# Local attention in a one-core hybrid block: scaling the output of a step instead of its probabilities

## The chip, the core and the metric

The kernel runs on one core of a Trainium2 chip. The metric is the device time of one execution in microseconds (us). Five engines work side by side, each with a queue of its own that runs in order: TensorE (PE in the profile; PEld is its loading of weights), VectorE (DVE), ScalarE (ACT), GpSimd (POOL) and SyncE (SP), which here only issues DMAs.

## The reference

One layer over 1024 latent tokens and 256 context tokens, width 1024, all in float32. A modulated norm feeds one projection; three token mixers work on it (A: attention in a window with a sink, B: global attention, C: a linear recurrence); their outputs are gated, merged and projected, and a gated MLP with a convolution follows. The change is in mixer A, with eight query heads of width 64 that share two key/value heads:

```python
s_loc = jnp.where(valid, s_loc, NEG_BIG)               # |kpos - qpos| <= 128
p = softmax(concatenate([s_ctx, s_loc, s_sink], -1))   # 256 context + up to 384 window keys + sink
o = p[..., :n_ctx] @ cv + p[..., n_ctx:-1] @ v_window  # the sink takes weight, gives no value
```

## The kernel before, in words

`attention` (L1229) runs once for mixer A (`br == 0`) and once for mixer B (`br == 1`). Each run has 16 steps: 8 blocks of 128 queries times 2 groups of 4 heads. In the trace mixer A's steps lie from about 697 to 889 us, mixer B's lead follows, and its steps end near 1222 us.

A step has three parts, which `weave` (L1214) interleaves in the order in which they are written down: `scores` of step it+1, `values` of step it, and a share of the gate projections (`gz`, L199 to L201), which need nothing of attention and fill TensorE. The framework's planner then orders each engine's queue from priorities and from times that it models. `qprep` (L1275) loads and transposes the queries two steps ahead.

- `softmax_window` (L1374) is the local `scores`. For each of four heads it makes five matmuls into a `sa` tile of PSUM (L1387 to L1392), takes the negative maximum (L1395, L1397), and writes `exp` to `pw` with its row sum (L1399). Then, per head (`NB = 1`, L68), it adds the sink's share to the sum (L1404 to L1406), takes the reciprocal (L1407), and GpSimd multiplies the whole 128x512 or 128x640 tile of probabilities by it (L1409).
- `softmax_global` (L1413) is mixer B's. It leaves its probabilities unscaled, makes one reciprocal per four heads, copies it out to 64 columns a head on GpSimd (L1450, tag `yT`) and puts that tile into `rs`.
- `values` (L1299) serves both. For each key tile, TensorE transposes four heads' probabilities into `pp` (L1321), a bank of the tag `a`; ScalarE makes the rounded half `ph` (L1325), VectorE the remainder `pl` (L1326), and two matmuls (L1307, L1308) add to `po`. At the end ScalarE copies the halves of `po` that have to change partitions (L1337, L1338), VectorE adds them to `yT` (L1341), and SP stores `yT` to DRAM (L1344). If `rs` has an entry for the step, two plain matmuls with the identity turn that tile into `pr`, also a bank of tag `a` (L1316), ahead of the third key tile; ScalarE copies `pr` to `ytmp` (L1318), and VectorE multiplies `yT` by it (L1343).

Tag `a` has two banks, shared by `pp`, `pr`, the turned queries `pq` (L1286) and, in a lead, `kt`. Tags `yT` and `ytmp` have two buffers each. The loads of keys and values for mixer B (L1251) stand behind mixer A's last store in SP's queue.

Of the kernel before, what the change touches and what calls it, by code (L numbers as in the profile page):

```python
# [12 lines left out]
AF = mybir.ActivationFunctionType  # L13
ALU = mybir.AluOpType
# [4 lines left out]
P = 128  # L19
# [48 lines left out]
NB = 1  # L68
# [1160 lines left out]
def attention(tc, nc, ap_, br, ins, kv_d, q_d, y_d, mm2, bank, ident, identr, fill_gen, fill_steps):  # L1229
    V, A, G, T, SP = nc.vector, nc.scalar, nc.gpsimd, nc.tensor, nc.sync  # L1230

    def tl(shape, tag, nm, bufs=2, dt=F32):
        return ap_.tile(shape, dt, tag=tag, name=f"{tag}{br}_{nm}", bufs=bufs)

    NK = 10
    KH = tl([P, 2, NK * P], "KH", 0, 1, F32R)
    KL = tl([P, 2, NK * P], "KL", 0, 1, F32R)
    VHL = tl([P, NK, 2, 2, 64], "VHL", 0, 1, F32R)
    if br == 0:
        tri = tl([P, 3 * P], "tri", 0, 1, F32)  # L1240
        SP.dma_start(tri, ins["tri"])
        trir = tl([P, 3 * P], "trir", 0, 1, F32R)
        A.copy(trir, tri)
        snk = tl([P, 8], "snk", 0, 1)
        SP.dma_start(snk, ins["sink"].to_broadcast([P, 8]))
        nsnk = tl([P, 8], "nsnk", 0, 1)
# [44 lines left out]
    def scores(it):  # L1291
        tt, g = divmod(it, 2)
        QT = QTs.pop(it)
        if br == 0:
            yield from softmax_window(nc, tl, mm2, tt, g, f"{it}_", QT, KH, KL, trir, identr, snk, nsnk, res)
        else:
            yield from softmax_global(nc, tl, mm2, g, f"{it}_", QT, KH, KL, res, rs)

# [49 lines left out]
    res, rs = {}, {}  # L1348
    def lead():
        for k0 in range(0, NK, 2):  # L1350
            prep(k0)
            yield
        qprep(0)
        qprep(1)
        yield
        yield from scores(0)
# [6 lines left out]
    for it in range(n_it):  # L1363
        PT, kts = res.pop(it)
        if it + 2 < n_it:
            qprep(it + 2)
        a, b = (min(fill_steps, int(fill_steps * i / (n_it - SKEW[br]))) for i in (it, it + 1))
        weave((scores(it + 1), S_LEN * (4 + br)) if it + 1 < n_it else (None, 0),
              (values(it, PT, kts), len(kts) + 1),
              (some(fill_gen, b - a), b - a))  # L1370
    man.close()


def softmax_window(nc, tl, mm2, tt, g, nm, QT, KH, KL, trir, identr, snk, nsnk, res):  # L1374
    V, A, G, T = nc.vector, nc.scalar, nc.gpsimd, nc.tensor
    lo, hi = max(tt - 1, 0), min(tt + 1, LT - 1)
    kts = [0, 1] + [2 + b for b in range(lo, hi + 1)]
    nk = len(kts) * P
    w = nk - 256
    m0 = (lo - (tt - 1)) * P  # L1380
    Ps = []
    st = tl([P, 8, 4], "st", nm)
    ng, sm, sk = st[:, 0], st[:, 1], st[:, 2]
    for h in range(4):

        sc = mm2(f"sa{nm}{h}").rearrange("p a b -> p (a b)")[:, 256:256 + nk]
        T.matmul(sc[:, :256], QT[:, h], KH[:, g, :256], start=True, stop=False)  # L1387
        T.matmul(sc[:, :256], QT[:, h], KL[:, g, :256], start=False, stop=True)
        k = (2 + lo) * P
        T.matmul(sc[:, 256:], QT[:, h], KH[:, g, k:k + w], start=True, stop=False)  # L1390
        T.matmul(sc[:, 256:], QT[:, h], KL[:, g, k:k + w], start=False, stop=False)
        T.matmul(sc[:, 256:], identr, trir[:, m0:m0 + w], start=False, stop=True)  # L1392
        n1 = ng[:, h:h + 1]
        hs = g * 4 + h
        V.tensor_reduce(out=n1, in_=sc, axis=AX.X, op=ALU.max, negate=True)  # L1395

        V.tensor_tensor(out=n1, in0=n1, in1=nsnk[:, hs:hs + 1], op=ALU.min)  # L1397
        pw = tl([P, 640], "pw", f"{nm}{h}", 8)
        A.activation(pw[:, :nk], sc, AF.Exp, bias=n1, accum_out=sm[:, h:h + 1])  # L1399
        Ps.append(pw)  # L1400
        if h % NB == NB - 1:
            b = slice(h - NB + 1, h + 1)
            bs = slice(hs - NB + 1, hs + 1)
            V.tensor_tensor(out=sk[:, b], in0=snk[:, bs], in1=ng[:, b], op=ALU.add)  # L1404
            A.activation(sk[:, b], sk[:, b], AF.Exp)
            V.tensor_tensor(out=sm[:, b], in0=sm[:, b], in1=sk[:, b], op=ALU.add)  # L1406
            V.reciprocal(sm[:, b], sm[:, b])  # L1407
            for j in range(h - NB + 1, h + 1):
                G.tensor_scalar(out=Ps[j][:, :nk], in0=Ps[j][:, :nk], scalar1=sm[:, j:j + 1], scalar2=1.0,  # L1409
                                op0=ALU.mult, op1=ALU.mult)  # L1410
        yield
    res[2 * tt + g] = ((lambda h, n: Ps[h][:, n * P:(n + 1) * P]), kts)


# [162 lines left out]
```

## Time and profile before

| | us |
|---|---|
| median of 3 runs (2128.03 to 2130.79) | 2129.37 |
| the profiled execution | 2129.82 |
| its span in the profile | 2127.9 |
| TensorE busy in the span | 2085.8 (98%) |
| GpSimd busy in the span | 288.1 (14%) |

Busy times of matmuls overlap, since a matmul begins before the one ahead of it has drained: read the distance from start to start beside them. "Idle before" is the gap of an engine, with the instruction that ended it.

### The profile page before, as it was taken

To read this page: it belongs to the slowest core of one execution; us is meant where nothing else is said; L and a number is where in the kernel's file an instruction comes from. 1 tells how busy PE (TensorE), PEld (TensorE's weight loads), DVE (VectorE), ACT (ScalarE), POOL (GpSimd) and SP (SyncE) were. 2 spreads that over 40 slices of the span, in tenths; PEclk is the share of its full clock that TensorE was granted. 3 is DMA by queue.
4 is the path that set the end of the run, shared out by engine and by line. 5 is a ranking of instruction groups with operands and counts; after the bars stand their busy time and mean duration, and the time that the engine had idled before them with its cause. 6 is when DMAs were issued, how large, how long until landed. Compare 5 with 4: busy or idle time off the path is not lost.

```text
span 2127.9 us, 30555 instructions
## 1 busy us (share of the span) xinstructions
PE 2085.8 (98%) x11686; PEld 1743.1 (82%) x11686; DVE 1380.5 (65%) x2299; ACT 1001.2 (47%) x1761; POOL 288.1 (14%) x257
## 2 busy tenths in 40 slices
PE   7999999999999999999999999999999999999997
PEld 4888888888988888878888788888888888888887
DVE  4736756636665777678887746569777777664423
ACT  4333333311123777678888734346445544453222
POOL 0000000010021222100000000011333344100111
PEclk9999999999999999999999999999999999999999
DMA  9511111136543211211100354641222222285342
GB/s 359 207 44 36 46 50 41 46 113 214 186 137 123 78 59 41 80 55 35 35 28 28 115 200 142 194 156 55 99 79 89 80 80 88 81 287 201 109 126 86
DMA packets 95490, 229.28 MB, mean 108 GB/s; under 512 B 10736, under 2 KB 35824, under 8 KB 94320
## 3 DMA queue, kind: packets, MB, share of 16 engines
q1 hardware_dynamic: 95344, 227.33, 32.1%
q8 instruction: 92, 1.51, 0.3%
q14 instruction: 54, 0.44, 0.1%
HBM read 181.68 MB, written 45.61 MB: 107 GB/s over the span
## 4 chain that ended last, share of the span: by engine, by line
PE 69%; DVE 3%; ACT 2%; issue 1%; DMA 1%; POOL 1%; SPq 0%; DVEq 0%; ACTq 0%; POOLq 0%
PE pp L1321 4%; PE gz L199 3%; PE dn L929 3%; PE dn L928 3%; PE dn L930 3%; PE gz L200 3%; PE gz L201 3%; PE up L852 2%; PE up L853 2%; PE up L854 2%; PE po L1307 2%; PE po L1308 2%; PE br L200 2%; PE br L201 2%; PE br L199 2%; PE upd L853 2%
## 5 line engine op out<-in xcount | busy, mean ns | idle before, releaser
L175 ACT CAST wh<-wr 128x1024 fp32r<-128x1024 f32 (+1 forms) x139 | 145.1, 1044 | 398.7 <-PE dn L929 69.1
L176 DVE TENSOR_TENSOR wl<-wr,wh 128x1024 fp32r<-128x1024 f32 (+1 forms) x139 | 171.1, 1232 | 221.1 <-ACT wh L175 206.7
L1326 DVE TENSOR_TENSOR pl<-pp,ph 128x512 fp32r<-128x512 f32 x236 | 159.3, 687 | 29.2 <-ACT ph L1325 23.5
L199 PE MATMUL gz<-hh,wh 128*128 128x512 f32 x384 | 156.3, 408 | 3.1 <-ACT gs L523 3.1
L1325 ACT CAST ph<-pp 128x512 fp32r<-128x512 f32 x236 | 135.7, 587 | 37.4 <-PE pp L1321 35.3
L201 PE MATMUL gz<-hh,wl 128*128 128x512 f32 x384 | 152.3, 397 | 0.0
L200 PE MATMUL gz<-hl,wh 128*128 128x512 f32 x384 | 152.1, 396 | 0.0
L210 PE MATMUL tm<-wl,hh 128*128 128x256 f32 x384 | 108.9, 283 | 3.3 <-DVE wl L176 3.3
L209 PE MATMUL tm<-wh,hh 128*128 128x256 f32 x384 | 108.9, 284 | 0.9 <-ACT qo L615 0.9
L211 PE MATMUL tm<-wh,hl 128*128 128x256 f32 x384 | 108.6, 283 | 0.0
L1307 PE MATMUL po<-ph,VHL 128*128 128x512 f32 x236 | 106.1, 450 | 1.4 <-ACT ph L1325 1.0
L929 PE MATMUL dn<-ac,wh 128*128 128x512 f32 x256 | 99.7, 390 | 0.0
L930 PE MATMUL dn<-ac,wl 128*128 128x512 f32 x256 | 99.6, 389 | 0.0
L928 PE MATMUL dn<-ac,wh 128*128 128x512 f32 x256 | 99.6, 390 | 0.0
L1308 PE MATMUL po<-pl,VHL 128*128 128x512 f32 x236 | 97.1, 411 | 0.1
L199 PEld LDWEIGHTS gz<-hh,wh 128*128 128x128 f32 x384 | 72.7, 189 | 17.2 <-ACT gs L523 5.2
L201 PEld LDWEIGHTS gz<-hh,wl 128*128 128x128 f32 x384 | 72.5, 189 | 15.0
L200 PEld LDWEIGHTS gz<-hl,wh 128*128 128x128 f32 x384 | 72.8, 190 | 11.6
L210 PEld LDWEIGHTS tm<-wl,hh 128*128 128x128 f32 x384 | 73.7, 192 | 4.3 <-DVE wl L176 4.0
L1321 PE MATMUL pp<-ident,plat 128*128 128x128 f32 x512 | 76.6, 273 | 0.0
L1321 PEld LDWEIGHTS pp<-ident,plat 128*128 128x128 f32 x512 | 62.7, 140 | 16.9 <-DVE pl L1326 1.2
L199 PE MATMUL br<-yh,wh 128*128 128x512 f32 x192 | 74.3, 390 | 1.6 <-ACT yh L1468 1.6
(1420 smaller groups left out, 5898.7 us busy)
## 6 DMA issues: line engine op xcount, KB each, us to landing
wr<-in_w_cm SPq DMA_DIRECT2D x48, 512.0 KB, 3.7
wr<-in_w_up SPq DMA_DIRECT2D x44, 512.0 KB, 3.5
wr<-in_w_down SPq DMA_DIRECT2D x33, 512.0 KB, 3.5
wmr<-in_w_mod SPq DMA_DIRECT2D x32, 512.0 KB, 4.5
gate_d<-gs SPq DMA_DIRECT2D x48, 256.0 KB, 2.3
sgt<-gate_d SPq DMA_DIRECT2D x24, 512.0 KB, 3.4
act_d<-u SPq DMA_DIRECT2D x22, 512.0 KB, 2.6
st<-act_d SPq DMA_DIRECT2D x44, 256.0 KB, 4.5
```

Of the source, the lines that this page charges most:

```text
L175: A.copy(hi[:, :n], raw[:, :n])
L176: (lo_eng or V).tensor_tensor(out=lo[:, :n], in0=raw[:, :n], in1=hi[:, :n].bitcast(F32), op=ALU.subtract)
L199: T.matmul(psl, wh[:, k, c], hh[:, k0 + k, cols], start=s, stop=False)
L200: T.matmul(psl, wh[:, k, c], hl[:, k0 + k, cols], start=False, stop=False)
L201: T.matmul(psl, wl[:, k, c], hh[:, k0 + k, cols], start=False, stop=e)
L210: T.matmul(psl, hh[:, k, toks], wl[:, k % 4, :], start=False, stop=False)
L928: T.matmul(z, w[0][:, c], h[0], start=s, stop=False)
L929: T.matmul(z, w[0][:, c], h[1], start=False, stop=False)
L930: T.matmul(z, w[1][:, c], h[0], start=False, stop=e)
L1307: T.matmul(po, vv, ph, start=n == 0, stop=False)
L1321: T.transpose(pp[:, h], PT(h, n), ident)
L1326: V.tensor_tensor(out=pl, in0=pp, in1=ph.bitcast(F32), op=ALU.subtract)
```

## The change: what it does

Local attention leaves its probabilities unscaled, as mixer B does. The sink's exponential, the addition and the reciprocal run once for four heads on 128x4 tiles; the reciprocal is copied out on GpSimd and put into `rs`. `values` is unchanged as text, and takes its `rs` path for mixer A too.

```diff
-            yield from softmax_window(..., snk, nsnk, res)
+            yield from softmax_window(..., snk, nsnk, res, rs)
...
         A.activation(pw[:, :nk], sc, AF.Exp, bias=n1, accum_out=sm[:, h:h + 1])
         Ps.append(pw)
-        if h % NB == NB - 1:
-            b = slice(h - NB + 1, h + 1)
-            bs = slice(hs - NB + 1, hs + 1)
-            V.tensor_tensor(out=sk[:, b], in0=snk[:, bs], in1=ng[:, b], op=ALU.add)
-            A.activation(sk[:, b], sk[:, b], AF.Exp)
-            V.tensor_tensor(out=sm[:, b], in0=sm[:, b], in1=sk[:, b], op=ALU.add)
-            V.reciprocal(sm[:, b], sm[:, b])
-            for j in range(h - NB + 1, h + 1):
-                G.tensor_scalar(out=Ps[j][:, :nk], in0=Ps[j][:, :nk], scalar1=sm[:, j:j + 1], scalar2=1.0,
-                                op0=ALU.mult, op1=ALU.mult)
         yield
+
+    V.tensor_tensor(out=sk, in0=snk[:, g * 4:g * 4 + 4], in1=ng, op=ALU.add)
+    A.activation(sk, sk, AF.Exp)
+    V.tensor_tensor(out=sm, in0=sm, in1=sk, op=ALU.add)
+    V.reciprocal(sm, sm)
+    rb = tl([P, 4, 64], "yT", f"r{nm}")
+    G.tensor_copy(rb, sm[:, :, None].to_broadcast([P, 4, 64]))
+    rs[2 * tt + g] = rb.rearrange("p a b -> p (a b)")
     res[2 * tt + g] = ((lambda h, n: Ps[h][:, n * P:(n + 1) * P]), kts)
```

## Rows read from the trace of the kernel before

**Rows 1.** The page, part 1: busy us, share of the span, instructions.

```profile
PE 2085.8 (98%) x11686; PEld 1743.1 (82%) x11686; DVE 1380.5 (65%) x2299; ACT 1001.2 (47%) x1761; POOL 288.1 (14%) x257
```

**Rows 2.** Busy time by stretch; the header names the columns.

```profile
core 0: us, PE busy (x) PEld busy (x) DVE busy (x) ACT busy (x) POOL busy (x), PEclk, DMA share, GB/s
697.00:706.00 9.00, 8.49 (x51) 7.01 (x50) 3.97 (x14) 6.43 (x15) 0.71 (x1) 1.00 0.35 116
706.00:730.00 24.00, 23.69 (x141) 19.36 (x140) 19.05 (x65) 18.31 (x50) 8.06 (x11) 1.00 0.23 67
730.00:874.00 144.00, 143.26 (x858) 124.41 (x857) 114.52 (x345) 104.65 (x264) 38.08 (x48) 1.00 0.16 49
874.00:886.00 12.00, 10.79 (x63) 8.56 (x61) 9.21 (x27) 8.91 (x23) 2.78 (x4) 1.00 0.21 47
888.00:892.00 4.00, 4.00 (x19) 3.33 (x18) 0.85 (x2) 0.42 (x1) 0.00 (x0) 1.00 0.41 130
908.00:927.00 19.00, 17.48 (x92) 13.57 (x91) 11.38 (x18) 13.93 (x29) 0.40 (x1) 1.00 0.17 56
```

**Rows 3.** Timeline of TensorE in mixer B, around a `pr` without a wait: start, us.

```profile
926.87 0.40 PE L199 MATMUL gz<-hh,wh 128*128 128x512 f32 x1
927.10 0.61 PE L1316 MATMUL pr<-ident,yT_r__8966 128*128 128x128 f32 x4
927.46 0.48 PE L1308 MATMUL po<-pl,VHL 128*128 128x512 f32 x1
927.78 0.60 PE L1321 MATMUL pp<-ident,plat 128*128 128x128 f32 x4
```

**Rows 4.** Groups of instructions by line, 697 to 889 us: busy, mean ns, idle before.

```profile
L1321 PE MATMUL pp<-ident,pw 128*128 128x128 f32 x304 | 47.3, 274 | 1.0 <-ACT QT L1288 0.7
```

**Rows 5.** Timeline of mixer A, TensorE at the end of a step.

```profile
743.26 0.28 PE L1388 MATMUL sa<-KL,QT 128*128 128x256 f32 x1
743.73 0.55 PE L1321 MATMUL pp<-ident,pw 128*128 128x128 f32 x3 [0.18 <-ACT QT L1288]
```

**Rows 6.** Waits of TensorE's weight loads, 697 to 889 us: total, times, longest.

```profile
PEld pp L1321 <- ACT QT L1288: 1.6, 4, 0.4
PEld pp L1321 <- POOL pw L1409: 1.1, 4, 0.3
```

**Rows 7.** Instructions of one step or one kind: min/median/max ns, first and last start.

```profile
L1409 POOL TENSOR_SCALAR pw<-pw,st__6758 x4: 799/808/812, 747.4 to 753.1; 128x640 f32<-128x640 f32 x4
L1407 DVE RECIPROCAL st__6758<-st__6758 x4: 149/158/165, 747.1 to 752.8; 128x1 f32<-128x1 f32 x4
L1407 DVE RECIPROCAL st__8168<-st__8168 x4: 151/157/164, 853.7 to 859.4; 128x1 f32<-128x1 f32 x4
L1405 ACT ACTIVATE st__6758<-st__6758 x4: 199/202/212, 745.5 to 752.3; 128x1 f32<-128x1 f32 x4
L1450 POOL COPY yT_r__8966<-st__8871 x1: 397/397/397, 924.5 to 924.5; 128x256 f32<-128x256 f32 x1
L1318 ACT COPY ytmp_R<-pr x16: 366/373/382, 929.6 to 1204.8; 128x256 f32<-128x256 f32 x16
L1343 DVE TENSOR_TENSOR yT<-yT,ytmp_R x16: 414/418/426, 943.7 to 1221.4; 128x256 f32<-128x256 f32 x16
```

**Rows 8.** Timeline of TensorE in mixer B, around a `pr` that waits for its bank.

```profile
1073.42 0.39 PE L201 MATMUL gz<-hh,wl 128*128 128x512 f32 x1
1074.10 0.68 PE L1316 MATMUL pr<-ident,yT_r__10632 128*128 128x128 f32 x4 [0.29 <-DVE pl L1326]
1074.54 0.48 PE L1307 MATMUL po<-ph,VHL 128*128 128x512 f32 x1
```

**Rows 9.** Timeline, last step of mixer A and SP's next issue.

```profile
879.12 0.19 ACT L1399 ACTIVATION_READ_ACCUMULATOR pw<-sa,st__8469 128x1 f32 x1
...
879.99 0.69 POOL L1409 TENSOR_SCALAR pw<-pw,st__8469 128x512 f32<-128x512 f32 x1 [1.49 <-DVE st__8469 L1407]
...
880.37 1.13 PE L1321 MATMUL pp<-ident,pw 128*128 128x128 f32 x8
880.66 1.05 ACT L175 CAST wh<-wr 128x1024 fp32r<-128x1024 f32 x1
...
882.24 0.50 PE L1307 MATMUL po<-ph,VHL 128*128 128x512 f32 x1 [0.74 <-ACT ph L1325]
...
888.91 0.37 SPq L1344 DMA_DIRECT2D y_d<-yT  x1
889.37 0.96 SPq L1251 DMA_DIRECT2D qf_kv<-kv_d  x2
```

More of the change, by code (lines that the diff above doesn't have):

```diff
@@ L1294, in scores @@
         if br == 0:
-            yield from softmax_window(nc, tl, mm2, tt, g, f"{it}_", QT, KH, KL, trir, identr, snk, nsnk, res)
+            yield from softmax_window(nc, tl, mm2, tt, g, f"{it}_", QT, KH, KL, trir, identr, snk, nsnk, res, rs)
         else:
@@ L1371, in attention, with softmax_window @@
     man.close()
-def softmax_window(nc, tl, mm2, tt, g, nm, QT, KH, KL, trir, identr, snk, nsnk, res):
+def softmax_window(nc, tl, mm2, tt, g, nm, QT, KH, KL, trir, identr, snk, nsnk, res, rs):
     V, A, G, T = nc.vector, nc.scalar, nc.gpsimd, nc.tensor
```

## The prediction, made before the result was known

> **What bounds the kernel now.** I read the page's busy shares first, then busy time by stretch for the part of the trace that holds mixer A, then who waits for whom there, and last the timeline of TensorE, start to start.
>
> Over the whole span TensorE is busy 98% and GpSimd 14% [rows 1]. The stage that the change touches is no exception. From 730 to 874 us, some twelve of the sixteen steps, TensorE is busy 143.26 of 144 us; with the stretches ahead and behind, idle time from 697 to 886 us comes to 0.51 + 0.31 + 0.74 + 1.21 = 2.8 us [rows 2]. VectorE is at 80% there, ScalarE at 73%, GpSimd at 26%. The granted clock is 1.00 in every stretch, the 2.4 GHz level, so the clock plays no part.
>
> Busy alone doesn't prove a full engine, since matmuls overlap in the record. So I looked at distances. A 128x512 matmul that waits for nothing starts 0.23 us after the one ahead of it [rows 3], and 144 us of mixer A's timeline, read start to start, leave some 11 us over such bare distances. More than half of that is a fixed 0.08 to 0.09 us whenever a 128x512 matmul follows a group of 128x128 ones (0.32 instead of 0.23 us, [rows 3]), and such groups come about six to a step (304 transpositions of `pp` in fours make 76 in 16 steps, the turned queries 16 more, [rows 4]). Real waits are rare: the largest that recurs is 0.36 us, four times, where a transposition finds its bank still held by the turned queries (0.47 us from start to start where 0.11 us is bare, [rows 5]). GpSimd's multiply, the piece that goes, held up weight loads by 1.1 us in all, four times [rows 6], and I found no matmul waiting for it. So mixer A's stage is bound by the amount of work in TensorE's queue, and what matters is whether the change adds to that queue.
>
> One rule speaks against this reading. The Trainium skill's Perfetto Trace Analysis (section Identifying the Most-Contended Engine) says that matmul busy share is a poor measure of headroom and that the share of weight loading should be used. By that rule the added matmuls would cost nothing. Weight loading is busy 124.41 of 144 us, 86%, from 730 to 874 us; but from 888 to 892 us, where only gate matmuls run and none waits, it is 3.33 of 4 us, or 83% [rows 2]. A full queue of this kernel shows no more than that, so the trace bears the rule out poorly here; what it would give is the second rival below.
>
> **The change part by part.**
>
> *Removed from the side engines.* Sixty-four multiplies of 0.69 to 0.81 us on GpSimd (3.2 us a step); per step three of four exponentials on ScalarE (3 x 0.20 = 0.6 us) and nine of twelve small VectorE instructions (9 x 0.155 = 1.4 us) [rows 7]. None is on the path that sets the end, since TensorE doesn't wait for them apart from the 1.1 us named.
>
> *Added beside TensorE.* Per step one broadcast copy on GpSimd, 0.40 us; one ScalarE copy of `pr`, 0.37 us; one VectorE multiply, 0.42 us [rows 7]. ScalarE and VectorE both end with less to do than before (by 0.2 and 1.0 us a step). These cost nothing while TensorE's queue has filler ahead; without that cover they would be 1.2 us a step.
>
> *Added to TensorE.* Per step two identity matmuls, which the trace shows as four instructions. In mixer B, where the same lines already run, such a group takes 0.36 us from its start to the next start, and the matmul behind it then takes 0.32 instead of 0.23 [rows 3]: 0.45 us a step, times 16 = 7.2 us. Nothing hides it, because TensorE has no gap to put it in.
>
> *A wait added.* `pr` takes one of the two `a` banks. Behind it in TensorE's queue stand the products and filler of the same step. In mixer B the group follows at the bare distance in 8 of its first 15 places; in 4 it comes about 0.17 us late, in 3 about 0.45 us late with the rest of the wait inside the group (0.44 instead of 0.36) [rows 8]. That is 2.6 us over 15, or 0.17 us a group, up to 2.7 us for 16. The lower end is zero. Mixer A would use 7 bank turns in a step of 11.8 us (nine steps from 747.1 to 853.7) against 12 in one of 18.5 us (fifteen from 943.7 to 1221.4) [rows 7], so nearly as dense; I take half, 1.3 us.
>
> *Is the reciprocal in time?* Behind the last exponential come its accumulator read, one small exponential, an addition, a reciprocal and the copy: 0.20 + 0.20 + 0.15 + 0.16 + 0.40 = 1.1 us [rows 7], plus hand-offs. `pr` is written down after two key tiles, each of which holds its bank for about 2 us through the two splits. So I charge nothing for it; if it came late, it would block the queue.
>
> *What may be won.* In the last step the probabilities of the fourth head are ready at 879.31, but GpSimd's multiply ends at 880.68; eight transpositions hold TensorE from 880.37 to 882.24, about 1.1 us longer than they need, because the split comes behind a weight cast on ScalarE [rows 9]. An earlier start could slip ahead of that cast: from 0 to 1.7 us counting the gap after it, and I take 1.0. The four bank waits of 0.36 us [rows 5] hang on ScalarE's queue, which gets a little shorter: 0 to 1.4 us, I take 0.7.
>
> *Handed on.* The last store now comes 0.42 us later, behind the new multiply, and the loads for mixer B follow it in SP's queue [rows 9]. The filler covers most of mixer B's lead, but it ends with TensorE idle for 1.5 us [rows 2], so the delay may come through: 0 to 0.5, I take 0.4. The stores of the other steps have a step's time to spare, and mixer A's output is read much later.
>
> Sum: 7.2 + 1.3 - 1.0 - 0.7 + 0.4 = +7.2 us on the profiled execution's 2129.8, so 2137.0 us. The median of the runs is 0.4 us lower, well inside their spread of 2.8.
>
> **The rivals.**
>
> 1. *The hand-off was the bound* (ends faster). If steps were paced by the chain from exponential through GpSimd to transposition, each would shorten by the multiply's 0.8 us, 12.9 us in all: 2117 us. It wins once more than 0.45 us a step of TensorE's time is really waiting. For it: the chain is long, and the matmul ends in the record are modelled. Against it: 2.8 us idle in 189, and filler that needs nothing of it.
>
> 2. *TensorE has room* (no change). If the modelled ends of matmuls hide gaps, the weight loads, one to a matmul, leave 19.6 us free in 144 [rows 2], and 7.2 us fit in; the 2.8 us idle could go too: 2127 to 2130 us. This is what the page named above would make of it. Against it stands that the stretch without waits looks the same.
>
> 3. *A better order pays half back.* The planner's order changes everywhere in mixer A. If two of five transposition groups then ran back to back, as they do in a few places, 2 x 0.09 x 16 = 2.9 us of switches would go, and with all waits recovered the sum is 7.2 - 2.9 - 1.7 = +2.6: 2132.4 us. Nothing in the profile says the order will be better rather than worse.
>
> 4. *`pr` blocks in each step.* At mixer B's worst place the group costs 0.45 of wait, 0.44 of its own and 0.09 behind, 0.98 us [rows 8]; times 16 that is +15.7: 2145.5 us. For it: two banks, in-order queues, and ScalarE's copy of `pr` holding up the next split. Against it: mixer B shows it in 3 of 15.
>
> **How the numbers follow.** Forecast 0.62, with a range of its own from 2134 to 2141; rival 1 0.05; rival 2 0.08; rival 3 0.15; rival 4 0.10. What a measurement tells from no change is about 0.2%, or 4.3 us, so faster means under 2125.1 and slower over 2133.6. Rival 1 gives 0.05 for faster. Rival 2, nearly all of rival 3 and a sliver of the forecast make 0.23 for no change; the rest, 0.72, is slower. The range for 8 in 10 leaves out rivals 1 and 2 mostly and the far end of 4: 2130.5 to 2142.
>
> **What the profile after would show.** Right: GpSimd busy in mixer A's stage falls from some 50 to under 10 us; 16 groups of L1316 stand in it, each 0.36 to 0.44 us start to start; TensorE still without gaps, and the stage from the first `sa` to the last `po` longer by 6 to 8 us, all other stages as long as before. Wrong: the stage's length unchanged or shorter with TensorE's idle time gone (rivals 1 and 2), or L1316 in mixer A with waits of over 0.3 us in most steps (rival 4), or a lead of mixer B that is longer by more than 1 us.

## The result and the profile after

The kernel after takes 2139.03 us (median of 6 runs, 2136.07 to 2141.7) against 2128.64 us for the kernel before beside it (6 runs, 2126.57 to 2130.79): a ratio of 1.0049 [1.0039, 1.0059], slower. The profiled execution took 2136.46 us, its span 2134.3 us. The forecast was 2137.0.

Part 1 of the page after, to be held against [rows 1], says at once which engine got more and which got less:

```profile
PE 2093.6 (98%) x11750; PEld 1749.2 (82%) x11750; DVE 1374.9 (64%) x2171; ACT 1001.1 (47%) x1729; POOL 243.6 (11%) x209
```

GpSimd lost 44.5 us of work, VectorE 5.6, ScalarE nothing. TensorE got 64 instructions more (16 groups of four) and 7.8 us of busy time, and the span grew by 6.4.

Next the busy time by stretch of the kernel after, with the columns of [rows 2]; the last row is new, since the stage now ends some 10 us later:

```profile
697.00:706.00 9.00, 9.00 (x57) 7.62 (x56) 4.75 (x13) 7.01 (x17) 0.00 (x0) 1.00 0.29 88
706.00:730.00 24.00, 23.67 (x147) 20.32 (x147) 18.79 (x45) 17.36 (x42) 1.21 (x3) 1.00 0.20 66
730.00:874.00 144.00, 142.71 (x850) 121.47 (x850) 102.44 (x230) 100.17 (x229) 4.43 (x11) 1.00 0.16 46
874.00:886.00 12.00, 11.94 (x73) 10.13 (x72) 8.38 (x23) 6.91 (x19) 0.40 (x1) 1.00 0.08 25
886.00:896.00 10.00, 8.69 (x47) 6.76 (x47) 6.01 (x11) 5.74 (x13) 0.40 (x1) 1.00 0.29 92
```

GpSimd is almost gone from mixer A's stage: 6.4 us in five stretches, against 49.6 in the first four of [rows 2]. TensorE's queue is as full as before, idle for 3.0 us in all. VectorE is at 71% instead of 80% in the middle stretch, and nothing came of it.

The steps' pace is read from the one reciprocal that each now has (min/median/max ns, first and last start, shapes); the two are nine steps apart:

```profile
L1406 DVE RECIPROCAL st__6571<-st__6571 x1: 168/168/168, 741.0 to 741.0; 128x4 f32<-128x4 f32 x1
L1406 DVE RECIPROCAL st__7909<-st__7909 x1: 168/168/168, 854.7 to 854.7; 128x4 f32<-128x4 f32 x1
```

That is 113.7 / 9 = 12.6 us a step, against (853.7 - 747.1) / 9 = 11.8 in [rows 7]: the loss is spread over the steps, not one stall.

To see where the span's 6.4 us lie, I cut the trace by two lines that begin and end the attention stages: the first `kt` (L1270) and the last gate matmul (L199). First the kernel before, then the one after (ns, first and last start):

```profile
L1270 PE MATMUL kt<-identr,qs_kk x80: 222/249/283, 685.2 to 905.9; 128*128 128x128 f32 x80
L199 PE MATMUL gz<-hh,wh x384: 387/393/628, 392.4 to 1198.0; 128*128 128x512 f32 x192
```

```profile
L1270 PE MATMUL kt<-identr,qs_kk x80: 220/250/286, 683.4 to 915.3; 128*128 128x128 f32 x80
L199 PE MATMUL gz<-hh,wh x384: 387/393/500, 392.4 to 1204.2; 128*128 128x512 f32 x192
```

Both attention stages together take 1198.0 - 685.2 = 512.8 us before and 1204.2 - 683.4 = 520.8 after: 8.0 us more. Behind them the rest is equally long (first `br` to the end of the span: 923.3 and 923.5 us). Ahead of them the kernel after came 1.8 us earlier, in code that is the same in both: the execution of before was granted the 1.2 GHz level for a part of these two windows, where the one after kept 2.4 GHz in both (before first, then after):

```profile
594.00:600.00 6.00, 3.77 (x17) 2.92 (x16) 3.37 (x9) 1.34 (x3) 1.54 (x1) 0.88 0.67 205
600.00:610.00 10.00, 10.00 (x60) 8.86 (x60) 4.82 (x8) 1.92 (x3) 0.10 (x1) 0.90 0.28 78
```

```profile
594.00:600.00 6.00, 4.48 (x23) 3.58 (x22) 3.30 (x9) 1.27 (x3) 1.55 (x1) 1.00 0.66 201
600.00:610.00 10.00, 10.00 (x72) 9.31 (x71) 5.59 (x10) 2.20 (x4) 1.01 (x1) 1.00 0.46 150
```

From 594 to 600 us TensorE was idle for 2.2 us, against 1.5 after. So the span hides 1.8 of the loss, and the stage's 8.0 us is the number to explain.

Now the distances in mixer A. A `pr` that doesn't wait, in the timeline of TensorE after:

```profile
743.41 0.39 PE L201 MATMUL gz<-hh,wl 128*128 128x512 f32 x1
743.64 0.61 PE L1316 MATMUL pr<-ident,yT_r__6688 128*128 128x128 f32 x4
744.00 0.47 PE L1307 MATMUL po<-ph,VHL 128*128 128x512 f32 x1
744.31 0.39 PE L1308 MATMUL po<-pl,VHL 128*128 128x512 f32 x1
```

It is mixer B's pattern of [rows 3] to the hundredth: 0.23 ahead, 0.36 for the group, 0.31 for the matmul behind it. Twelve of the 16 groups look so. The other four have transpositions of `pp` right behind them:

```profile
755.64 0.40 PE L201 MATMUL gz<-hh,wl 128*128 128x512 f32 x1
755.87 0.61 PE L1316 MATMUL pr<-ident,yT_r__6841 128*128 128x128 f32 x4
756.41 0.66 PE L1321 MATMUL pp<-ident,pw 128*128 128x128 f32 x4
```

Here 0.54 us pass instead of 0.36. Ahead of all 16 groups stands only the bare distance: not one waits for its bank as in [rows 8].

Start to start, mixer A's stage (first `sa` to last `po`) goes from 187.2 to 197.6 us, mixer B's lead (from there to the first matmul of its scores) from 22.2 to 22.5, mixer B (from there to the last gate matmul) from 288.9 to 286.4. The filler in mixer A is nearly the same (260 gate matmuls before, 262 after). The 10.4 us in mixer A are: 5.6 for the 16 bare groups, 1.0 for the four long ones and small delays, 1.1 for the 0.09 us behind the twelve others, 0.5 for the four waits on the turned queries, 0.5 for the two gate matmuls that came over from mixer B, and 1.7 in small differences over many places that I can't give to one cause. Mixer B gives 2.5 back. The largest part is one wait in its first scores, which both executions of the kernel before have (the first here, then the second, which is run again below) and neither of the kernel after; why it goes isn't shown. The waits of TensorE from 886 to 920 us (total, times, longest):

```profile
PE sbl L1435 <- ACT pc__8872 L1428: 1.5, 1, 1.5
PE sbl L1435 <- ACT pc__8872 L1428: 1.7, 1, 1.7
```

### The profile page after: what moved, and what is told of

It reads as the page before. It is cut to its first block, busy times and chain, and to the rows that moved or that the text cites. A ratio compares the mean times of both kernels' runs of the same rounds, so it can differ in the third digit from the quotient of the medians.

```text
span 2134.3 us, 30376 instructions
## 1 busy us (share of the span) xinstructions
PE 2093.6 (98%) x11750; PEld 1749.2 (82%) x11750; DVE 1374.9 (64%) x2171; ACT 1001.1 (47%) x1729; POOL 243.6 (11%) x209
## 4 chain that ended last, share of the span: by engine, by line
PE 54%; ACT 1%; DVE 1%; DMA 1%; issue 1%; POOL 0%; SPq 0%; DVEq 0%; ACTq 0%
PE pp L1321 3%; PE dn L929 3%; PE dn L928 3%; PE dn L930 3%; PE up L852 2%; PE up L853 2%; PE up L854 2%; PE br L200 2%; PE br L201 2%; PE br L199 2%; PE po L1307 2%; PE upd L854 2%; PE upc L854 2%; PE upc L853 2%; PE upd L853 2%; PE upd L852 2%
## 5 line engine op out<-in xcount | busy, mean ns | idle before, releaser
L199 PE MATMUL gz<-hh,wh 128*128 128x512 f32 x384 | 155.9, 407 | 2.4 <-ACT gs L523 2.4
L199 PEld LDWEIGHTS gz<-hh,wh 128*128 128x128 f32 x384 | 72.3, 188 | 15.7 <-ACT gs L523 4.3
L209 PEld LDWEIGHTS tm<-wh,hh 128*128 128x128 f32 x384 | 73.6, 192 | 2.6 <-ACT qo L615 2.2
```

What stands on the lines that cost most here:

```text
L199: T.matmul(psl, wh[:, k, c], hh[:, k0 + k, cols], start=s, stop=False)
L209: T.matmul(psl, hh[:, k, toks], wh[:, k % 4, :], start=s, stop=False)
```

## The experiments

The theory: TensorE's queue is full, so the identity matmuls are paid at their start-to-start time, once for each, wherever the rest of the change goes. Rivals: the side engines' new instructions or the later store cost it; the bank wait costs it; or the lighter GpSimd is worth something and hides a larger loss. Runs of one batch were timed beside the kernel before on the same chip. The recorded expectations give the attention stages up to the end of the last gate matmul, some 0.4 us more than the figures here.

**The same kernel again.** No edit.

> The changed kernel once more, beside the kernel before on the same chip, to narrow the size of the loss. From the two traces the attention stages grew by 8.0 us (513.1 to 521.2 us between the first turned keys of mixer A and the last gate matmul), while the medians differ by 10.4 us. Theory (TensorE's queue got more work): 8 to 9 us over the kernel before, ratio 1.0038 to 1.0042. If something outside the attention stages costs time too, the ratio stays at 1.0049 or more.

2137.91 us (5 runs), 1.005 [1.0037, 1.0062]; span 2132.9, attention stages 521.3 us. The loss repeats, and at 10.0 us it is more than the 8 to 9 that I expected: by my own words something outside the attention stages would cost time too. This trace shows nothing of the kind. Behind them the rest takes 923.4 us, as in the other two traces.

**Without the output's scaling.**

```diff
-    rb = tl([P, 4, 64], "yT", f"r{nm}")
-    G.tensor_copy(rb, sm[:, :, None].to_broadcast([P, 4, 64]))
-    rs[2 * tt + g] = rb.rearrange("p a b -> p (a b)")
```

> The changed kernel without the reciprocal's way to the output: no copy to 64 columns, no pr, no copy of pr, no final multiply, so mixer A's output stays unnormalised. All that was removed from the side engines stays removed. Theory (queue work): the whole loss goes, since the pr groups, the switches behind them and their bank are what costs: within 2 us of the kernel before, ratio 0.999 to 1.001. Rival (the hand-off through GpSimd had been the bound, and its relief hides part of the cost): clearly under the kernel before, by 5 us or more. Rival (a worse order of the queues costs): still 4 us or more above it.

2130.85 us (11 runs), 1.0013 [1.0004, 1.0022]; attention stages 511.3 us. The loss is mostly gone, though the 3.0 us that are left are more than the 2 I allowed. Nor is the kernel faster than before, although three of four small exponentials, nine of twelve small VectorE instructions and all of GpSimd's multiplies have gone from each step with nothing in their place. So the multiplies cost nothing where they were.

**The matmuls twice.** In mixer A the same two matmuls are issued again into the same tile.

```diff
+                for _ in range(2 if br == 0 else 1):
                     for a in range(2):
                         T.matmul(pr[:, a], r[:, a * P:(a + 1) * P], ident, start=True, stop=True)
```

> The changed kernel with mixer A's two identity matmuls issued twice into the same bank, so 16 more groups of four instructions and nothing else. Theory (queue work): each group costs its bare 0.35 us, no new switch: 5.6 us over the changed kernel, 16 over nothing hidden; ratio to the kernel before 1.0065 to 1.0075. Rival (the loss comes from waits: the bank, ScalarE's copy, the order of the buffers): under 2 us more than the changed kernel, since a longer pr meets the same waits.

2142.73 us (5 runs), 1.0069 [1.0056, 1.0081], 4.8 us over the kernel after in the same batch; attention stages 527.3, 6.0 over. The timeline of TensorE at the same step as above (in this kernel line numbers from `pr` on are one higher):

```profile
745.09 1.05 PE L1317 MATMUL pr<-ident,yT_r__6694 128*128 128x128 f32 x8
745.90 0.47 PE L1307 MATMUL po<-ph,VHL 128*128 128x512 f32 x1
746.21 0.39 PE L1308 MATMUL po<-pl,VHL 128*128 128x512 f32 x1
```

The group takes 0.81 us instead of 0.36, so 16 x 0.45 = 7.2, and here the switch behind it is paid once, as before. (In eleven of the 16 steps transpositions stand right behind the group, and it takes 0.89 to 0.95.) Mixer A's stage grew by 6.2 us, the medians by 4.8. So most of what the second pair occupies is paid, with no new side work. The rival wanted under 2.

**The added way on top of the kernel before.** The three lines of `rb` and the argument `rs` are put into the kernel before, whose probabilities stay scaled, so the output is scaled twice.

> The kernel before with only the additions: probabilities are still scaled per head on GpSimd, and the reciprocal is also copied out, turned by two identity matmuls per step and multiplied into the output, which is so scaled twice. Theory (queue work, side engines free of charge): the same loss as the changed kernel, 7 to 10 us, ratio 1.0033 to 1.0047, for the removed side work was worth nothing. Rival (the relief of GpSimd, ScalarE and VectorE was worth something): slower than the changed kernel by 3 us or more, ratio over 1.006.

2138.34 us (5 runs), 1.0051 [1.0039, 1.0064]; attention stages 520.9. It is as slow as the kernel after, though it keeps all that the change removes. So what was removed was worth nothing that these runs can tell, and what was added makes the whole loss by itself. The size lies a little over the upper end of what I expected.

**Four heads at once on GpSimd.** In the kernel before.

```diff
-NB = 1
+NB = 4
```

> The kernel before with one part of the change alone: sink and sums once for four heads, while GpSimd still multiplies the probabilities, now four tiles in a row at the end of the heads. TensorE gets no new work. Theory (queue work): within 2 us of the kernel before, ratio 0.999 to 1.001, the saved small instructions being worth nothing. Rival (the hand-off from softmax to transposition matters): slower by 3 us or more, since the first head's probabilities come later.

2155.14 us (4 runs), 1.0131 [1.0112, 1.0151]; attention stages 535.7. This expectation failed. The waits of TensorE between 697 and 912 us (total, times, longest) and those of its weight loads name the cause; in [rows 6] the second line had 1.1 us:

```profile
PE pp L1321 <- POOL pw L1409: 12.9, 25, 1.3
PEld pp L1321 <- POOL pw L1409: 31.4, 56, 1.5
```

And busy time in the middle of the stage, where TensorE now stands idle for 9 of 144 us:

```profile
730.00:874.00 144.00, 135.05 (x752) 106.96 (x751) 101.24 (x206) 90.34 (x203) 37.83 (x44) 1.00 0.15 46
```

The timelines of GpSimd and of TensorE in it:

```profile
756.53 3.13 POOL L1409 TENSOR_SCALAR pw<-pw,st__6710 128x640 f32<-128x640 f32 x4 [9.77 <-PE po L1308]
```

```profile
757.41 0.31 PE L1321 MATMUL pp<-ident,pw 128*128 128x128 f32 x1
758.16 0.33 PE L1321 MATMUL pp<-ident,pw 128*128 128x128 f32 x1 [0.44 <-POOL pw L1409]
758.94 0.33 PE L1321 MATMUL pp<-ident,pw 128*128 128x128 f32 x1 [0.21 <-POOL pw L1409]
```

The four multiplies stand in a row of 3.1 us at the start of `values`, and each transposition follows its head's multiply: 0.75 and 0.78 us apart where 0.09 is bare. So the hand-off that rival 1 had in mind does exist; head by head, as in the kernel before, it is early enough and off the path, and it comes onto it as soon as the multiplies come in one block behind the fourth head's sum. The same pooling of sink and sums is harmless in the kernel after because no probability waits for it any more.

**Transpositions in place of the identity matmuls.** Both mixers of the kernel after, then mixer B of the kernel before (mixer A has none there).

```diff
-                    T.matmul(pr[:, a], r[:, a * P:(a + 1) * P], ident, start=True, stop=True)
+                    T.transpose(pr[:, a], r[:, a * P:(a + 1) * P], ident)
```

> The changed kernel with the two identity matmuls of a step replaced by two transpositions, in mixer A and in mixer B: two instructions instead of four a step. Theory (queue work): a transposition of 128x128 starts 0.09 us before the next, so each group shrinks from 0.36 to 0.18 us, 32 groups give 5.7 us: 2132 to 2133 us, still 3 to 5 us over the kernel before. Rival (the loss comes from waits around pr and its bank): under 2 us less than the changed kernel.

> The kernel before with transpositions instead of identity matmuls for mixer B's reciprocals. Theory (queue work): 16 groups give 0.18 us each, 2.8 us: ratio 0.9985 to 0.999, so a version that beats both. Rival (mixer B's groups hide behind waits for their bank): no difference, ratio 0.9995 to 1.0005.

The first takes 2130.49 us (11 runs), 1.0007 [0.9998, 1.0016] of before; attention stages 514.8, against 520.8 and 521.3 of the kernel after. The second takes 2123.14 us (9 runs), 0.9975 [0.9966, 0.9985], and beats both kernels; attention stages 508.4. The group in mixer A of the first, then one in mixer B of the second, both in TensorE's timeline:

```profile
745.78 0.38 PE L1316 MATMUL pr<-ident,yT_r__6688 128*128 128x128 f32 x2
745.92 0.48 PE L1307 MATMUL po<-ph,VHL 128*128 128x512 f32 x1
```

```profile
1068.86 0.39 PE L201 MATMUL gz<-hh,wl 128*128 128x512 f32 x1
1069.09 0.38 PE L1316 MATMUL pr<-ident,yT_r__10632 128*128 128x128 f32 x2
1069.23 0.48 PE L1307 MATMUL po<-ph,VHL 128*128 128x512 f32 x1
```

Two instructions instead of four, 0.14 us instead of 0.36. The second group is the one of [rows 8]: there it came 0.68 us behind the matmul ahead of it and took 0.44, here 0.23 and 0.14. I had counted the shorter group alone, and that at 0.18 us less. Start to start, the 16 places of `pr` in mixer B take 5.3 us less: 16 x 0.22 = 3.5 for the instructions, the other 1.8 for waits around them (the waits view names one wait of `pr` for its bank, of 1.0 us, where the kernel before has four, of 1.8 us in all). The stages got shorter by 4.4 us, or 3.7 against the second execution of the kernel before; the medians say 5.7.

The Trainium skill says it as a rule (Perfetto Trace Analysis, Transposes): "Ensure logical transpose operations use transpose, as opposed to a standard matmul." The rows agree: 0.22 us less for each pair of this size.

Held against each other, the two kernels say what the change costs once both mixers turn by transposition: 7.4 us at the medians, 6.4 in the attention stages. The pair's own time is then only 16 x (0.14 + 0.09) = 3.7 us. Mixer A's stage is 7.7 us longer (187.2 and 194.9), of which 0.7 is three gate matmuls more. So some 3 us of the change's cost are neither the matmuls' own time nor the switch behind them, and these runs don't place them.

**The kernel before against itself.** No edit.

> The kernel before against itself, for a second profile of it and for the size of what the comparison can tell. Every theory: ratio 1 within 0.001. The attention stages, from the first turned keys of mixer A to the last gate matmul, 513 to 514 us again if the 8.0 us between the two traces are the change's; if they spread by 2 us or more, the difference between the traces' 8 us and the medians' 10 us is the spread of single executions.

2129.54 us (11 runs), 1.0004 [0.9995, 1.0014]; attention stages 512.1 us. A difference of 0.1% is no difference here. The stages are 0.7 us shorter than in the first execution, so the traces put the change at 8.0 to 9.2 us (520.8 - 512.8 and 521.3 - 512.1).

**The side engines' part alone.** The kernel after without mixer A's two matmuls and their bank: ScalarE copies the tile unturned, so mixer A's output isn't scaled rightly.

```diff
+                if br == 1:
                     pr = bank("a", f"pr{br}{it}", (P, 2, P))
                     for a in range(2):
                         T.matmul(pr[:, a], r[:, a * P:(a + 1) * P], ident, start=True, stop=True)
+                else:
+                    pr = r.rearrange("p (a b) -> p a b", a=2)
```

> The changed kernel without the two identity matmuls and their bank in mixer A, but with everything else of the reciprocal's way: GpSimd copies it out, ScalarE copies that tile (unturned, so the scaling is not the reference's) into the place of the turned one, VectorE multiplies the output by it. Theory (only TensorE's work costs, the side engines' share is hidden): within 2 us of the kernel without the whole way, so 7 us or so under the changed kernel, ratio to the kernel before 0.999 to 1.002. Rival (ScalarE's copy, the multiply or the later store cost): 3 us or more over the kernel without the way, ratio 1.003 or more.

**Without the output's scaling, again**, beside it.

> The kernel without the reciprocal's way once more: its median was 3.0 us over the kernel before (1.0013), while its attention stages in the profile were 1.6 us shorter (511.7 against 513.3 us). If the first was the spread of executions, the ratio now comes out at 0.999 to 1.001; if unscaling alone costs some 3 us by something that the one profiled execution did not show, it is again 1.001 or more and the profile may show where.

2129.71 us (11 runs), 1.0005 [0.9996, 1.0014], and 2129.86 us (12 runs), 1.0006 [0.9997, 1.0015]. GpSimd's copy, ScalarE's copy, VectorE's multiply and the later store make no difference that these runs can tell; the two matmuls and their bank are most of the loss. They may not be all of it: the three runs without the pair lie 2.0 to 3.0 us over the kernel before, only the first of them clear of noise, and their mixer A took 187.6 to 189.0 us where the two executions of the kernel before took 186.6 and 187.2. That leaves 7 to 8 of the 10 us for the pair. The attention stages took 513.4 and 514.8 us. The second kernel is the one that took 511.3 us in the earlier batch. Its waits of TensorE from 697 to 930 us tell those two executions apart; neither line is there in the earlier one:

```profile
PE pq L1286 <- DVE qs_q L1282: 1.7, 2, 1.3
PE sbl L1430 <- ACT pc__8616 L1423: 1.4, 1, 1.4
```

One hangs on the queries' loads, the other on the lead of mixer B. They come and go between executions of one kernel, as the stretch of lower clock does.

## Why the prediction was right

Slower was right, inside the range, and in the main for the reason given: the groups cost the same in mixer A as in mixer B, and nothing hid them. The size was met less well, 10.4 us at the medians where 7.2 were forecast. Rule against row: weight loading is busy 121.47 of 144 us after, so 22.5 us would seem free, more than the 19.6 of before; yet the doubled matmuls were paid with 4.8 us at the medians and 6.0 in the traces, of 7.2. The Trainium skill says of TensorE to judge headroom by the share of peak arithmetic and of weight loading (Perfetto Trace Analysis, Identifying the Most-Contended Engine). The second of the two, as the prediction read it, counts room here that couldn't be used, as the stretch of gate matmuls alone in [rows 2] had said.

By its terms:

**Groups and switch, +7.2.** 5.6 + 1.1 = 6.7: right.

**Bank wait, +1.3.** 1.0 was found, but by another way than forecast: `pr` itself finds its bank free, and in four steps the `pp` behind it comes late. The waits of the weight loads, 697 to 897 us, have lines that fit, the first of them the copy that frees `pr`'s bank:

```profile
PEld pp L1321 <- ACT ytmp_R L1318: 1.3, 5, 0.3
PEld pp L1321 <- ACT QT L1288: 2.6, 4, 0.7
```

**Bank waits of the turned queries, -0.7.** The sign was wrong: the second line is 2.6 us where [rows 6] has 1.6. In the timeline after, the place that answers to [rows 5]:

```profile
741.62 0.34 PE L1391 MATMUL sa<-KL,QT 128*128 128x384 f32 x1
742.27 0.55 PE L1321 MATMUL pp<-ident,pw 128*128 128x128 f32 x3 [0.31 <-ACT QT L1288]
```

0.65 us where 0.17 is bare, so 0.48 instead of 0.36, four times. It isn't the work of `pr`: the kernels without it show the same 2.6 us. The kernel before with the added way, whose steps keep their old exponentials, sums and multiplies, shows the old figure (697 to 897 us):

```profile
PEld pp L1321 <- ACT QT L1288: 1.6, 4, 0.4
```

So it goes with what was removed. ScalarE had less to do and still came later; the changed order of its queue is my guess, and no run tests it.

**The last step, -1.0.** Nothing came. The timeline after that answers to [rows 9]:

```profile
887.89 1.04 PE L1321 MATMUL pp<-ident,pw 128*128 128x128 f32 x8
888.17 1.05 ACT L175 CAST wh<-wr 128x1024 fp32r<-128x1024 f32 x1
889.75 0.49 PE L1307 MATMUL po<-ph,VHL 128*128 128x512 f32 x1 [0.82 <-ACT ph L1325]
```

The weight cast still begins 0.28 us behind the transpositions, ahead of the split that they wait for, and 1.86 us pass to the next matmul where 1.87 did. The start that I hoped for, ahead of the cast by more than the split needs, didn't come about.

**The hand-off, +0.4.** Right, with 0.3 found. The last store stands behind the new multiply, as foreseen, and comes 2.6 us behind the last `po` (895.25), where it came 2.1 us behind it (886.81, and 888.91 in [rows 9]). Mixer B's lead is 22.5 us instead of 22.2 (23.1 and 22.1 in the second executions), and in it the turning of a key (L1270) now waits for ScalarE's copy. Multiply and store in the timeline after, then the wait of TensorE:

```profile
897.35 0.43 DVE L1343 TENSOR_TENSOR yT<-yT,ytmp_R 128x256 f32<-128x256 f32 x1
897.81 0.37 SPq L1344 DMA_DIRECT2D y_d<-yT  x1
```

```profile
PE kt L1270 <- ACT qs_kk L1261: 0.5, 1, 0.5
```

**Not foreseen:** the 2.2 us of small differences and moved filler in mixer A, and the 2.5 that mixer B gives back. By the first, mixer A's stage alone grew by 10.4 us, more than the 6 to 8 that I had named as a sign of being right; by the second, the other stages weren't as long as before, another of those signs.

Terms that were gains of the side engines were all wrong (-1.7 forecast, +0.5 found), and the sum in the traces, +8.0, came near +7.2 because the unforeseen terms cancel; that is luck. The medians say more, +10.4 with an interval of 8 to 13 us; the second run of the kernel agrees with both. Which part of the 2 us between trace and medians is the change and which is the scatter of single executions stays open. It isn't the clock: where the kernel after ran again, its 5 runs had the same mean granted clock as the 15 of the kernel before beside them, 0.9968.

Of the rivals, the hand-off as a bound (1) fell with the runs without scaling, which weren't below before, and room on TensorE (2) with the doubled matmuls. Of the better order (3) little came: beside the twelve behind `pr` there are 90 places in mixer A where a larger matmul follows a 128x128 group, against 96, where that rival wanted 32 fewer. The block in each step (4) showed in no step.

## What to carry to other kernels

Before moving work between engines, ask which queue is full start to start: 44 us taken from an engine at 14% bought nothing, and 16 groups of 0.36 us on the one at 98% cost 8 to 10, waits and order included. Once TensorE is the bound, look at what its small instructions are: two plain float32 matmuls with the identity took four instructions where two transpositions took two, and that single word made the version here that beats both kernels. And a chain that costs nothing can be one edit away from the path: pooling the sums of four heads, harmless after the change, cost 26 us while the probabilities still waited for them.

## What the runs showed of the hardware that was not expected

- Two transpositions of 128x128 float32 take 0.14 us start to start, two plain matmuls with the identity 0.36, at the same granted clock of 1.00.
- A shorter use of a shared PSUM bank gave back waits beside its own time: with transpositions in mixer B alone, the 16 places took 5.3 us less start to start, where 16 x 0.22 = 3.5 was the instructions' share.
- The same kernel's attention stages differed by 3.5 us between two executions (511.3 and 514.8), with single waits of 1.3 to 1.4 us on loads and leads in the longer one alone.
